# Two transformer blocks in one kernel: where the steps that make the modulation vectors are issued

## The chip, the core and the metric

The kernel runs on one core of a Trainium2 chip. The metric is device time in microseconds (us). Three runs of the kernel before took 2303.86, 2305.15 and 2305.77 us, so its median is 2305.15 us.

## The reference, cut to what matters

Two transformer blocks of two layers each run one after the other on 512 latent tokens of 1024 features (the first block also on 256 context tokens). Every layer begins with a norm whose result is scaled and shifted by *modulation vectors*, and ends with a gate that is one too. All modulation vectors come from one small vector `c` (in the first block also `c_ctx`) and large matrices, and depend on nothing else:

```python
for l in range(DEPTH):                    # first block
    mod_l = (silu(c) @ ada_w[l] + ada_b[l])           # [6 * 1024]
    mod_c = (silu(c_ctx) @ ada_w[l] + ada_b[l])
    sh1, sc1, g1, sh2, sc2, g2 = split(mod_l, 6)
    xl = xl + g1 * mixer(rms_norm(xl, norm_mix_w[l]) * (1 + sc1) + sh1)
    xl = xl + g2 * conv_ffn(rms_norm(xl, norm_ffn_w[l]) * (1 + sc2) + sh2)
for l in range(DEPTH):                    # second block
    sh, sc, g = split(silu(c) @ ada_w_2[l] + ada_b_2[l], 3)
    x = x + g * attention(rms_norm(x, norm_g_2[l]) * (1 + sc) + sh)
```

That makes 18 vectors of 1024 numbers: `(0, ...)` and `(1, ...)` with six names each for the first block's layers, `(2, ...)` and `(3, ...)` with sc, sh and g for the second block's. Those of layer 0, and (1, sc1) and (1, sh1), have two columns (`c` and `c_ctx`), the others one.

## The kernel before, in words

Tokens lie along the free dimension and features along the 128 partitions, in 8 chunks. All products are float32 made of two parts: a weight block and an activation are each split into a high part (wH, hH) and a low part (wL, hL), and TensorE adds up three products of them (L333).

**Weights.** They lie in DRAM in the order of their use, in blocks of 512 KB. `Stream.load` (L67 to L73) brings a block into one of 5 buffers of the tag `raw`; `Stream.prep` splits it, wH by ScalarE (L85) and wL by VectorE (L86), into one of 4 pairs. A block is split one block ahead of its use, and each split is followed by a further load. All loads are issued by SP, in one order.

**The stages, in order.** `mixer0`; `ffn(0)` on 768 tokens (feed-forward layer 0); `mixer1`; `ffn(1)` on 512 tokens (layer 1); `even2`, the first attention of the second block; `odd2`, the second. A feed-forward layer goes through the 2816 hidden features in three groups (8, 7, 7 blocks of 128): the up-projection `lin("up...")`, then the down-projection `lin("dn...")`. The last down-projection works by parts of the tokens, and as each part is done, the next layer's norm of that part follows (`norm`, `after`, L461 to L463: n_t and hL on VectorE, hH on ScalarE). The first two blocks of a layer's first product also go by parts. The attentions are 8 units each; `overlap` (L1065) emits unit i and, behind it in priority, the products that unit i + 1 needs. The softmax of a unit goes from TensorE (scores) to VectorE (L1139), ScalarE (L1140), VectorE (P, L1248 or L1287), TensorE (transposes, L1130) and both (ptH, ptL), then to TensorE again.

**The modulation vectors.** They are made in 144 steps. A step loads a tile of 512 KB of a matrix (`ada_load`, L242) into one of the same 5 `raw` buffers. The first 40 steps are done by TensorE in `mixer0` (`ada_pe`). The other 104 are those of the generator `ada` (L290): 13 vectors of 8 steps, with 4 steps for each half of a vector. A step holds two chunks of the matrix's rows. For each chunk ScalarE multiplies the tile by the chunk's scalars (L308, and L304 for a half's first chunk), and GpSimd adds it to an accumulator `gacc` (L309); where a vector has two columns, VectorE does the first column's part (L306). After the fourth step four small products for each column by TensorE sum over the partitions (L316), and VectorE turns the result (L318) and adds the bias (L257, L264).

**When a step is issued.** `mm` counts in `self.pe` TensorE's time as columns / 2400 us. `run` emits the work; behind each chunk of a product it asks whether `pe` has reached `ada_next`, and if so it emits a step and sets `ada_next = pe + every`. `ada_pace(9.2)` is set at a feed-forward layer's start (L699) and `ada_pace(inf)` at its end (L713), `ada_pace(11.0)` in `even2` (L1324), where it stays. `ada_until(keys)` emits at once the steps that are still missing for the vectors named: in `ffn` ahead of each down-projection (L706), in `even2` (L1326) and `odd2` (L1427) ahead of the last unit, there for (2, g), (3, sc), (3, sh) and for (3, g).

The order in which it is emitted is a priority: a scheduler orders every engine's instructions by it, as far as what each needs is there by its estimate. So a step's load or products can run well before the product behind which they were emitted. On the chip each engine then works in that fixed order.

```python
    def run(self, *gens):                              # L388
        for g in gens:
            for _ in g:
                while self.pe >= self.ada_next:
                    next(self.ada_gen, None)
                    self.ada_next = self.pe + self.ada_every
```

Of the kernel before, what the change touches and what calls it, by code (L numbers as in the profile page):

```python
# [21 lines left out]
KD = 8  # L22
# [4 lines left out]
NF = DFF // 128  # L27
# [20 lines left out]
class Stream:  # L48
    """Weight blocks in the order of their use, loaded ahead and split into two float32r parts."""
# [47 lines left out]
    def take(self, tag, ahead=None):  # L97
        """The next block's parts; the blocks behind it are made ready first."""
        i = self.used
        assert self.blocks[i][0] == tag, (tag, self.blocks[i])  # L100
        self.ahead(1)
        self.used += 1
        self.ahead(self.kk.AHEAD if ahead is None else ahead)
        return self.ready.pop(i)


class Banks:
    """A product's token runs, each in a bank of PSUM that is taken when it is first named."""
# [14 lines left out]
class Kern:  # L123
# [42 lines left out]
    def psum(self, parts, **banks):  # L166
        """Who takes which of the banks, in turn, from here on; parts: who, by part of the tokens."""
        self.banks, self.turn = {**self.BANKS, **banks}, dict.fromkeys(self.BANKS, 0)
        self.parts = parts
# [64 lines left out]
    def ada_load(self, pool=None, bufs=0):  # L234
        """Step (m, b, n, k, d): of vector m the blocks of 128 columns b .. b + n, of its matrix the rows k .. k + d."""
# [16 lines left out]
    def ada_put(self, m, b, n, value, nv):  # L252
        """The modulation vector's blocks b .. b + n have their product: value."""
# [15 lines left out]
    def ada_pe(self, n):  # L269
        """The next n steps of modulation vectors, by TensorE."""  # L270
# [19 lines left out]
    def ada(self):  # L290
        """The modulation vectors: sums over the chunks of the rows by GpSimd, over the partitions by TensorE."""
# [30 lines left out]
    def ada_pace(self, every):  # L322
        self.ada_every, self.ada_next = every, self.pe + every
# [12 lines left out]
    def lin(self, tag, nb, hH, hL, segs, evac, first=None, last=None, after=None):  # L336
        """Feature-major blocks: psum[m, t] = sum_k W[k, m] h[k, t]; the first or last two by parts of the tokens,
        after(part) when the last two have had one."""
# [27 lines left out]
    def lin_tm(self, tag, pairs, hH, hL, nt, evac):  # L366
        """Token-major blocks of 256 columns: psum[t, m] = sum_k h[k, t] W[k, m]."""
# [15 lines left out]
    def split(self, src, h, l):  # L383
        """h + l = src, each a float32r."""
# [3 lines left out]
    def run(self, *gens):  # L388
        """Emits the gens; among them, as TensorE's time passes, the modulation vectors' steps."""
        for g in gens:  # L390
            for _ in g:
                while self.pe >= self.ada_next:
# [4 lines left out]
    def merge(main, fill, per):  # L397
        """Runs main; behind each of its steps, fill's for about that much time on TensorE."""
# [10 lines left out]
    def pipeline(steps):  # L409
        """Steps of (elementwise, TensorE, what reads PSUM): each stage one step behind the one before."""  # L410
# [12 lines left out]

    def rsqrt(self, pool, r, x, n, scratch=None):
        """r = (x / n + eps) ** -0.5 =: v ** -0.5, by a step of Newton's: y (3 - 4 v y y), y about v ** -0.5 / 2."""
# [10 lines left out]
    def rstd_from(self, pool, rstd, sq, segs, n):  # L436
        """rstd[p, t] = (sum_p sq[p, t] / n + eps) ** -0.5 on all partitions."""
# [5 lines left out]
    def norm(self, name, side, T, x, A, B):  # L443
        """A modulated norm of x(j, s, e), by parts of the tokens: add() takes a chunk whose values are there, after()
        makes the part's H + L once all its chunks are."""
# [21 lines left out]
    def sumsq(self, pool, T, x):  # L467
        """add(j, s, e): takes chunk j's squares; rstd(part): the tokens' 1 / rms, on all partitions."""
# [174 lines left out]

    def ffn(self, l, T, segs, parts, n, x, nxt, side):
        """Adds to the chunks x(j, s, e); n: their norm; nxt opens the next layer's."""
# [53 lines left out]
        self.ada_pace(9.2)  # L699
# [19 lines left out]

    def mixer1(self, n):  # L720
# [19 lines left out]
        def raw_evac(raw, acc):  # L740
            """Copies block b to raw[b] and adds its squares to acc."""
# [63 lines left out]
    def out_proj(self, tag, y, gate, side, done, nxt):  # L805
        """x += gate * (y @ w); done: the pools to close when y has been split; nxt opens the next norm."""
# [21 lines left out]
    def rotate(self, pool, x, rope):  # L828
        """x: 64-feature heads [128, 512]; each pair of 16-feature runs turned by its angles."""
# [37 lines left out]
    def mla_in(self, tmp, keep, scratch, qlH, qlL, kvH, kvL, qp, rope):  # L867
        """The heads' queries, keys and values by token, the first two normalised but for their weights; qp[h]:
        the turned part of the queries, by feature, [high; low] or [low; high]."""
# [6 lines left out]
        def unit(*parts):  # L876
            """Each (x, nt, n): the heads of n features of nt tiles of tokens, over their rms."""
# [68 lines left out]
    def mla(self, raw, y, qpe, kpH, kpL, first):  # L946
# [8 lines left out]
        def weighted(h, x, nt, w, tag):  # L955
            """[tokens, 128] tiles -> w times their features by token, as a float32r pair: steps."""
# [107 lines left out]
    def overlap(self, n, produce, attend, first=(), last=None):  # L1064
        """Attends to unit i, behind it in priority what produces unit i + 1; last() before the last unit."""  # L1065
# [951 lines left out]
```

## Time and profile before

| | |
|---|---|
| median of three runs | 2305.15 us (2303.86 to 2305.77) |
| the profiled execution: span from first to last instruction | 2305.6 us |
| TensorE busy | 2199.9 us, 95% of the span |
| VectorE busy | 1542.2 us, 67% |
| ScalarE busy | 1118.7 us, 49% |
| GpSimd busy | 407.4 us, 18% |
| mean granted clock of TensorE | 0.985 |
| bytes read from HBM | 222.46 MB, 97 GB/s over the span |

What lies around the span is not shown apart: the span is within the three runs' times, 0.45 us above their median. A granted clock of 1.00 is 2.4 GHz, of 0.50 is 1.2 GHz. "PE" is TensorE's matmul, "PEld" its weight load, DVE is VectorE, ACT is ScalarE, POOL is GpSimd, SP issues the loads. A busy TensorE is not one at its peak: matmuls are pipelined, and their ends are modelled.

### The profile page before, as it was taken

The page shows a single profiled execution, that of the slowest core. Times are in us where ns is not written, and L with a number is a line of the kernel's source. Part 1 is how long each engine was busy: PE and PEld are TensorE (multiplying, and loading weights), DVE is VectorE, ACT ScalarE, POOL GpSimd, SP SyncE. Part 2 cuts the span into 40 slices and gives each one's busy share as a digit, 9 for nine tenths or more (in the row PEclk, how much of TensorE's full clock was granted, in tenths as well). Part 3 has the DMA queues.
Part 4 walks back from the last instruction along what each step waited for, and adds up shares of the span by engine and source line. Part 5 has one row for each costly group of instructions (what it writes and reads, how often), then busy time and mean ns, then how long its engine had stood idle before and what let it go on. Part 6 is the DMA issues. An engine that isn't in the chain of part 4 may idle for free.

```text
span 2305.6 us, 34273 instructions
## 1 busy us (share of the span) xinstructions
PE 2199.9 (95%) x13243; PEld 1880.2 (82%) x13243; DVE 1542.2 (67%) x2938; ACT 1118.7 (49%) x2124; POOL 407.4 (18%) x389
## 2 busy tenths in 40 slices
PE   6899899989999999999999999999999989989997
PEld 4788798788888888888889878878788877778886
DVE  5867775486545544547798675454567867968996
ACT  5444443254423423334577454343446756746773
POOL 0323321012122221221000013222211122101110
PEclk9999999999999999999999999999999999989999
DMA  9111111713333334331220134445434232213111
GB/s 322 65 47 32 33 56 38 283 56 125 106 117 110 113 107 128 105 115 59 76 92 1 46 119 138 145 131 155 137 108 137 80 95 92 73 56 95 56 46 37
DMA packets 86708, 226.78 MB, mean 98 GB/s; under 512 B 7184, under 2 KB 15376, under 8 KB 86544
## 3 DMA queue, kind: packets, MB, share of 16 engines
q1 hardware_dynamic: 86544, 224.58, 30.6%
q8 instruction: 104, 1.70, 0.3%
q14 instruction: 60, 0.49, 0.1%
HBM read 222.46 MB, written 2.10 MB: 97 GB/s over the span
## 4 chain that ended last, share of the span: by engine, by line
PE 75%; DVE 15%; ACT 5%; issue 2%; DMA 2%; POOL 1%; SPq 0%; DVEq 0%; ACTq 0%; POOLq 0%
PE b L333 72%; DVE wL L86 2%; DMA raw<-in_ada_w_dram 2%; DVE hL L463 1%; DVE n_t L461 1%; PE b L1130 1%; ACT wH L85 1%; PE b L280 1%; DVE s L1139 1%; DVE ptL L386 1%; PE b L1018 1%; DVE ksL L1092 1%; DVE n_acc L478 0%; PE b L316 0%; ACT ptH L385 0%
## 5 line engine op out<-in xcount | busy, mean ns | idle before, releaser
L333 PE MATMUL b<-hH,wH 128*128 128x256 f32 (+1 forms) x1880 | 597.6, 359 | 15.3 <-ACT hH L462 8.0
L333 PE MATMUL b<-hH,wL 128*128 128x256 f32 (+1 forms) x1880 | 593.5, 357 | 3.6 <-DVE wL L86 3.6
L333 PE MATMUL b<-hL,wH 128*128 128x256 f32 (+1 forms) x1880 | 588.9, 356 | 2.9 <-DVE hL L463 2.8
L309 POOL TENSOR_TENSOR gacc<-gacc,raw 128x512 f32<-128x512 f32 x182 | 261.5, 1437 | 1002.6 <-ACT raw L308 971.5
L333 PEld LDWEIGHTS b<-hH,wH 128*128 128x128 f32 x1880 | 356.0, 191 | 70.6 <-ACT hH L462 9.6
L333 PEld LDWEIGHTS b<-hH,wL 128*128 128x128 f32 x1880 | 357.6, 191 | 52.8 <-DVE wL L86 4.2
L333 PEld LDWEIGHTS b<-hL,wH 128*128 128x128 f32 x1880 | 355.5, 191 | 53.7 <-DVE hL L463 3.9
L86 DVE TENSOR_TENSOR wL<-raw,wH 128x1024 fp32r<-128x1024 f32 (+2 forms) x270 | 341.9, 1268 | 73.9 <-ACT wH L85 73.2
L85 ACT ACTIVATE wH<-raw 128x1024 fp32r<-128x1024 f32 (+2 forms) x270 | 278.1, 1031 | 176.0 <-PE b L333 173.4
L308 ACT ACTIVATE raw<-raw,csil 128x512 f32<-128x512 f32 x182 | 125.6, 717 | 202.4 <-DMA raw<-in_ada_w_dram 134.1
L333 PE MATMUL b<-hidH,wH 128*128 128x512 f32 (+1 forms) x563 | 167.8, 345 | 0.0
L333 PE MATMUL b<-hidH,wL 128*128 128x512 f32 (+1 forms) x563 | 167.4, 344 | 0.0
L333 PE MATMUL b<-hidL,wH 128*128 128x512 f32 (+1 forms) x563 | 167.2, 344 | 0.0
L333 PE MATMUL b<-yH,wH 128*128 128x256 f32 (+1 forms) x408 | 129.5, 334 | 5.1 <-ACT yH L385 4.9
L333 PE MATMUL b<-yH,wL 128*128 128x256 f32 (+1 forms) x408 | 129.5, 333 | 1.5 <-DVE wL L86 1.5
L333 PE MATMUL b<-yL,wH 128*128 128x256 f32 (+1 forms) x408 | 129.5, 334 | 0.0
L668 DVE TENSOR_SCALAR a<-gp,vecs 128x769 f32<-128x769 f32 (+1 forms) x44 | 39.1, 888 | 123.9 <-ACT gp L664 123.9
L333 PEld LDWEIGHTS b<-hidH,wH 128*128 128x128 f32 x563 | 105.5, 188 | 14.5 <-issue 1.2
L333 PEld LDWEIGHTS b<-hidH,wL 128*128 128x128 f32 x563 | 105.8, 188 | 13.6
L333 PEld LDWEIGHTS b<-hidL,wH 128*128 128x128 f32 x563 | 105.8, 188 | 13.1
L385 ACT ACTIVATE ptH<-b 128x384 fp32r<-128x384 f32 (+2 forms) x160 | 77.7, 500 | 64.7 <-PE b L1130 49.0
L333 PE MATMUL b<-wH,hH 128*128 128x256 f32 x352 | 100.9, 288 | 2.7 <-ACT z L519 1.5
(366 smaller groups left out, 3938.9 us busy)
## 6 DMA issues: line engine op xcount, KB each, us to landing
raw<-in_weights_dram SPq DMA_DIRECT2D x231, 512.0 KB, 3.5
raw<-in_ada_w_dram SPq DMA_DIRECT2D x144, 512.0 KB, 3.9
raw<-in_weights_dram SPq DMA_DIRECT2D x32, 448.0 KB, 3.3
x0t<-in_xT_dram SPq DMA_DIRECT2D x4, 768.0 KB, 7.0
xlat<-in_xT_dram SPq DMA_DIRECT2D x2, 1024.0 KB, 10.2
out_dram<-fo SPq DMA_DIRECT2D x8, 256.0 KB, 2.3
raw<-in_weights_dram SPq DMA_DIRECT2D x3, 384.0 KB, 3.0
xctx<-in_xT_dram SPq DMA_DIRECT2D x2, 512.0 KB, 7.0
```

What stands on the lines that cost most here:

```text
L85: nc.scalar.activation(h[:, :n], src, AF.Copy)
L86: nc.vector.tensor_tensor(l[:, :n], src, h[:, :n].bitcast(F32), op=ALU.subtract)
L280: nc.tensor.matmul(acc[32 * q:32 * q + 32, :], self.csil[:, k + a, :], raw[:, a, :, q, :], start=k + a == 0, stop=k + a == KD - 1)
L308: nc.scalar.activation(raw[:, a], raw[:, a], AF.Copy, scale=c)
L309: nc.gpsimd.tensor_tensor(acc[v], acc[v], raw[:, a], op=ALU.add)
L333: self.nc.tensor.matmul(ps, lhsT, rhs, start=start, stop=stop, **kw)
L385: self.nc.scalar.activation(h, src, AF.Copy)
L386: self.nc.vector.tensor_tensor(l, src, h.bitcast(F32), op=ALU.subtract)
L461: nc.vector.scalar_tensor_tensor(t, x(j, s, e), A[:, j, v:v + 1], r, op0=ALU.mult, op1=ALU.mult)
L463: nc.vector.scalar_tensor_tensor(hL[j][:, s:e], t, b, h.bitcast(F32), op0=ALU.add, op1=ALU.subtract)
L668: nc.vector.tensor_scalar(a, gp[:, 1:1 + L], cw(1, i), cb(i), op0=ALU.mult, op1=ALU.add)
L1018: nc.tensor.transpose(ps[:, c], P[:, a, c], self.ident)
```

## The change

In a feed-forward layer the pace is 7.2 in place of 9.2. The first step may come 8 us later than it could before, and none comes in the layer's last 16 us (by `self.pe`, and `total` is the layer's count). `even2` sets no pace any more, so that after layer 1 it stays at infinity, and only the demands of `ada_until` emit steps. Docstrings and comments also go, which changes no instruction.

```diff
-    def ada_pace(self, every):
-        self.ada_every, self.ada_next = every, self.pe + every
+    def ada_pace(self, every, start=0.0, end=math.inf):
+
+        self.ada_every, self.ada_next, self.ada_end = every, self.pe + start + every, self.pe + end
...
     def run(self, *gens):
...
         for g in gens:
             for _ in g:
-                while self.pe >= self.ada_next:
+                while self.ada_next <= self.pe < self.ada_end:
                     next(self.ada_gen, None)
                     self.ada_next = self.pe + self.ada_every
...
     def ffn(self, l, T, segs, parts, n, x, nxt, side):
...
-        self.ada_pace(9.2)
+        total = 3 * NF * KD * 3 * T / 2400
+        self.ada_pace(7.2, 8.0, total - 16.0)
         i0 = 0
...
     def even2(self, n):
...
-        self.ada_pace(11.0)
         def last():
             self.ada_until((2, "g"), (3, "sc"), (3, "sh"))
             self.close("h_b0")
```

## Rows read from the trace of the kernel before

**Rows 1.** Four stages: stretch, us, busy PE PEld DVE ACT POOL, granted clock, DMA share, GB/s
```profile
700.00:900.00 200.00, 200.00 (x1192) 174.47 (x1191) 94.36 (x106) 67.23 (x95) 47.99 (x33) 1.00 0.36 113
1500.00:1650.00 150.00, 150.00 (x665) 119.40 (x665) 79.80 (x90) 60.82 (x85) 35.37 (x24) 1.00 0.47 142
1760.00:2000.00 240.00, 228.20 (x1135) 180.56 (x1134) 191.91 (x405) 166.30 (x317) 45.89 (x30) 0.99 0.30 92
2060.00:2250.00 190.00, 188.51 (x1068) 157.72 (x1067) 173.38 (x509) 135.72 (x358) 25.97 (x48) 1.00 0.20 63
```

**Rows 2.** The additions of L309 alone in even2: stretch, us, POOL busy, clock, DMA
```profile
1745.00:2000.00 255.00, 39.09 (x28) 0.99 0.30 94
```

**Rows 3.** The chain of waits: a group of small products in layer 1
```profile
1374.72 0.36 PE b L316 x8
```

**Rows 4.** Who made TensorE wait from 1760 to 2010: us in total, times, longest
```profile
PE b L333 <- DVE sm L1139: 4.1, 2, 3.2
PE b L1130 <- DVE P L1287: 2.5, 4, 0.9
PE b L333 <- DVE vb L386: 1.7, 1, 1.7
PE b L1130 <- DVE sm L1281: 1.1, 1, 1.1
```

**Rows 5.** ScalarE's timeline in even2: start, us, operation [idle before <-releaser]
```profile
1891.56 0.72 ACT L308 ACTIVATE raw<-raw,csil 128x512 f32<-128x512 f32 x1 [2.19 <-DMA raw<-in_ada_w_dram]
```

**Rows 6.** Short stretches after TensorE's waits, columns as in rows 1
```profile
1344.00:1348.00 4.00, 1.88 (x8) 1.79 (x9) 3.93 (x11) 1.31 (x3) 0.00 (x0) 0.50 0.74 248
...
1722.00:1726.00 4.00, 4.00 (x20) 3.92 (x21) 4.00 (x12) 1.92 (x5) 0.00 (x0) 0.58 0.12 46
1865.00:1870.00 5.00, 4.09 (x16) 3.67 (x17) 4.43 (x15) 3.17 (x7) 0.81 (x1) 0.66 0.17 68
1890.00:1895.00 5.00, 3.27 (x9) 2.05 (x8) 1.61 (x4) 2.70 (x7) 1.26 (x1) 0.67 0.49 154
```

**Rows 7.** VectorE's timeline at five places, alone and beside GpSimd's additions
```profile
507.68 1.66 DVE L463 SCALAR_TENSOR_TENSOR hL<-n_t,mods,hH 128x256 fp32r<-128x256 f32 x4
...
1336.95 3.52 DVE L463 SCALAR_TENSOR_TENSOR hL<-n_t,mods,hH 128x256 fp32r<-128x256 f32 x4
...
1710.99 1.32 DVE L478 TENSOR_TENSOR n_acc<-n_acc,n_sq 128x256 f32<-128x256 f32 x1 [0.54 <-ACT n_sq L477]
...
1718.45 1.38 DVE L433 TENSOR_TENSOR rsz<-rsz,rsm 128x256 f32<-128x256 f32 x1
...
1729.31 0.41 DVE L432 TENSOR_TENSOR rsz<-n_r 128x256 f32<-128x256 f32 x1
...
1837.43 1.48 DVE L1287 SCALAR_TENSOR_TENSOR P<-P,sm 128x512 f32<-128x512 f32 x1
...
1928.13 0.74 DVE L1287 SCALAR_TENSOR_TENSOR P<-P,sm 128x512 f32<-128x512 f32 x1
```

**Rows 8.** TensorE's timeline: the first products after four waits
```profile
518.71 0.58 PE L333 MATMUL b<-hH,wL 128*128 128x256 f32 x1 [3.28 <-DVE wL L86]
...
1346.12 0.58 PE L333 MATMUL b<-hH,wH 128*128 128x256 f32 x1 [2.83 <-ACT hH L462]
...
1719.61 0.43 PE L316 MATMUL b<-gacc,ones 128*32 128x128 f32 x8 [0.66 <-POOL gacc L309]
1721.89 0.38 PE L333 MATMUL b<-hH,wH 128*128 128x256 f32 x1 [1.85 <-ACT hH L462]
```

**Rows 9.** SP's timeline: loads of modulation matrices at the layers' starts
```profile
471.93 0.38 SPq L242 DMA_DIRECT2D raw<-in_ada_w_dram  x1
...
1330.67 0.38 SPq L242 DMA_DIRECT2D raw<-in_ada_w_dram  x1
...
1344.23 0.38 SPq L242 DMA_DIRECT2D raw<-in_ada_w_dram  x1
```

**Rows 10.** DMA issues: operation xcount, KB each, median us from issue to landing
```profile
raw<-in_ada_w_dram SPq DMA_DIRECT2D x144, 512.0 KB, 3.9
```

## The prediction

> **What bounds the kernel now.** The table by stage comes first. From 700 to 900 us (feed-forward layer 0) and from 1500 to 1650 us (layer 1) TensorE has not one idle microsecond, though the modulation steps run there: no other engine is near its limit, and only what stops TensorE or lowers its clock costs time. From 1760 to 2000 us (the first attention of the second block, "even2") it idles 240 - 228.2 = 11.8 us, and steps run there too; in the second attention ("odd2", 2060 to 2250), built alike and without steps, 1.5 us in 190 [rows 1]. After that I read who makes TensorE wait [rows 4], what the queues of ScalarE and VectorE do just before those waits [rows 5, 7], and the same at layer 1's two ends, where a norm ties TensorE to VectorE: there it idles again, and the granted clock falls to 0.5, the 1.2 GHz level [rows 6, 8].
>
> A step is a 512 KB load by SP, two products on ScalarE, two additions on GpSimd; every fourth adds a group of small products on TensorE.
>
> **How many steps go where.** The emitter counts TensorE's time in chunks, of 0.96 us in layer 0 and 0.64 in layer 1, so a pace of 9.2 becomes 9.6 in both (10 and 15 chunks), and 7.2 becomes 7.68 (8 and 12). Of 144 steps, 40 are done ahead of layer 0. Before: 53 in layer 0 (52 by the pace, one by the demand ahead of the last down-projection), 35 in layer 1, 16 in even2. The trace agrees: 28 additions from 1745 to 2000 us [rows 2], and four half vectors have 7 each. After: layer 0 counts 506.88 us; its first step comes at 15.36 (8.0 + 7.2, up to the next chunk) and the last before 490.88, which makes 62. Layer 1 counts 337.92 us, from 15.36 to 321.92: 40. That is 102 of 104. The last two, of the vector (3, g), are left to the demand ahead of odd2's last unit. So +9, +5, -16, and +2 in odd2, which had none: the change does not quite do what its name says.
>
> **even2.** Three things go with its 16 steps. (1) ScalarE's queue is in order: before 1891.56 a step's product had made it wait 2.19 us for its landing, the copies of vb stood behind it [rows 5], and TensorE waited 1.7 us for vb [rows 4]. (2) GpSimd's additions stretch VectorE: a 512-column update of P takes 0.74 us alone and 1.48 beside an addition, 0.74 more [rows 7]. (3) Four groups of products, 0.36 us each on the chain [rows 3], 1.4 in all. The waits that I tie to steps, since an addition or a landing stands beside the last links before them, are those for sm of L1139, P, vb and sm of L1281: 4.1 + 2.5 + 1.7 + 1.1 = 9.4 us [rows 4], 80% of the 11.8. The two longest lower the clock: 0.66 and 0.67 in two stretches of 5 us, 3.3 us lost, of which some 0.9 falls on idle already counted: 2.4 [rows 6]. I take 9.4 and 80% of the 2.4, less 0.5, since odd2 has some idle too: 10.8, with the groups **-12.2**. Bounds: all of it, -11.8 - 2.4 - 1.4 = -15.6, and +1 (the same idle for other reasons, in a new order of instructions).
>
> **End of layer 1.** Two steps run while the last down-projection turns into the next norm. Beside their additions three short operations of VectorE take about 1.35 us each (first and third shown: 1.32, 1.38), where 0.41 is usual: 2.8 us on the chain that TensorE waits for [rows 7]. It idles 0.66 us for an addition itself and 1.85 for the norm [rows 8], then runs at clock 0.58 for 4 us, 1.7 us lost [rows 6]. Now the last step comes 24 us of TensorE time before the layer's end, not 3. What is late next is the norm's second half, VectorE's work in one piece; so I gain what VectorE gains, 2.8, and some of the clock: **-3.5**. Bounds: 0, and -(0.66 + 1.85 + 1.7 + 0.36) = -4.6.
>
> **Start of layer 1.** The first step's load is issued at 1330.67 [rows 9]; its additions stretch four hL from 1.66 to 3.52 us [rows 7], and TensorE then waits 2.83 us [rows 8] and falls to clock 0.50 [rows 6]. In the new order this step stands behind one more weight block: the first two end at 10.24 us, the third at 15.36. SP takes the steps' and the weights' loads in one order, so the load goes about where the second step's went, 1344.23 [rows 9]. VectorE gains 1.9 us and ScalarE a little: **-2.2**. Bounds: 0, and the wait with half of the 1.88 us that ran at half clock, -2.83 - 0.9 = -3.8.
>
> **Start of layer 0.** Here the 8 us buy nothing. Steps 1 to 4 stood at 9.6, 19.2, 28.8 and 38.4 us, within blocks 0-1, 2, 3 and 4; now they stand at 15.36, 23.04, 30.72 and 38.4, the ends of the same blocks. Each load follows the same weight load as before, and the first goes out at 471.93, ahead of the layer [rows 9]. So the additions stay where they are, and so does the wait of 3.28 us for a weight's low part [rows 8]: **0**. Bounds: -5 (this wait, and a clock loss like the 1.7) and +1.9 (one more pair of additions, as at layer 1's start). At layer 0's end the norm has no addition beside it: 0.
>
> **Inside the layers.** 14 more steps are 3.5 groups of 0.36 us [rows 3]: **+1.3**, since TensorE is full. The loads, products and additions I cost at nothing: in 200 us of layer 0 VectorE is busy 94.4, ScalarE 67.2, GpSimd 48.0 [rows 1]. In layer 0's up-projections a step now falls on every block's end; one in four or five did before, without a wait. If that cover is gone, see the first rival.
>
> **odd2.** Two steps, where VectorE is busy 173.4 of 190 us [rows 1]. Their loads wait in SP's order behind the output projection's first blocks, and put its last ones off; those are needed last. Price of a step in even2: (11.8 + 2.4) / 16 = 0.9; two of them and a group, 1.8 + 0.4: **+2.2**. Bounds: 0.4, and both landings exposed at 3.9 us each with the group, 8.2 [rows 10].
> The Trainium skill (SBUF — State Buffer, section "Who interferes with whom") holds that only the port pair which VectorE and GpSimd share causes contention, and that it is an exclusive lock. By that rule an addition can hold VectorE for its whole 1.3 us or so, not 0.74 as the row has it; four of them would make the odd2 term up to 5.2 + 0.4, and the sum 2294.
>
> **The sum.** -12.2 - 3.5 - 2.2 + 0 + 1.3 + 2.2 = -14.4. The profiled execution's span is 2305.6 us, 0.45 above the median of the runs (2305.15): 2305.6 - 14.4 - 0.45 is 2290.75, say **2291**.
>
> **Rivals.**
> *The layers can't hide it (slower).* Steps and weights share five load buffers and SP's one order, so a step that is late delays weights. If a block's low part then comes late in layer 0, TensorE waits as it does at 518.71, 3.28 us [rows 8]. This outweighs the gain from (14.4 + 1.3) / 102 = 0.15 us a step; at 0.3, one such wait in eleven steps, it adds 31: 2322. Against it: no idle at all in the 200 us of layer 0 or the 150 us of layer 1 [rows 1]. 8%.
> *even2's idle is not the steps'.* VectorE and ScalarE hand each softmax to and fro, and one wait would come for another. Then 1.4 of the 12.2 is won: 2291 + 10.8 = 2302. For it: each of these waits names VectorE's own softmax work, not a step [rows 4]. Against it: odd2 idles little. 18%.
> *odd2 pays in full.* Both landings fall on the last unit: 8.2 in place of 2.2, 2297. For it: VectorE has little slack there; against: the output projection's blocks are there to fill TensorE. 12%.
>
> **How the numbers follow.** The forecast keeps 62%. A measurement of this kernel tells some 0.2%, 4.6 us; the second rival, 3 us under the median, lies within that, with half its chance on either side. Faster: 0.62 x 0.98 + 0.18 x 0.5 + 0.12 x 0.85 = 0.80; same: 0.01 + 0.08 + 0.02 = 0.11; slower: the first rival and a little, 0.09. Range: even2, layer 1's ends and layer 0's start at the better bounds give -3.4 - 1.1 - 1.6 - 5; not all come together, and 10 of these 11 make 2281. The high end takes in the other two cases: 2302.
>
> **What would show it.** Right: short VectorE operations at layer 1's end and no addition there; no step in even2, idle there under 4 us and no half clock; a first wait in layer 1 under 1 us; layer 0's start as it is; two steps in odd2 before its last unit. Wrong: waits for wL or for evacuations inside the layers, or idle of 8 us and more in even2 without steps.

## The result, and the profile after

The changed kernel takes 2337.89 us (median of 4 runs, 2332.78 to 2339.23) against 2305.46 for the kernel before on the same chip: 1.3% slower, ratio 1.0132 with a 95% interval of 1.0117 to 1.0146. The forecast was 2291, 0.6% faster. The profiled execution took 2339.23 us, its span is 2337.5 us.

To see where the time went I cut both spans at five marks on GpSimd, which stand at the same places of the work: the clearing of layer 0's buffers (gp), the first sum of squares of mixer 1 (kvr), the clearing of layer 1's buffers, the first bias made from dist (even2) and the first from band (odd2).

| stage | before, us | after, us | difference | predicted |
|---|---|---|---|---|
| layer 0, to mixer 1's first sum | 592.8 | 627.4 | **+34.6** | +0.8 |
| mixer 1 | 252.6 | 252.7 | +0.1 | 0 |
| layer 1, to even2's bias | 408.5 | 413.3 | **+4.8** | -5.2 |
| even2, to odd2's bias | 344.8 | 333.1 | -11.7 | -12.2 |
| odd2, to the end | 218.3 | 221.8 | +3.5 | +2.2 |

(0.8 and -5.2 divide the +1.3 inside the layers by steps, 9 to 5.) What was to be gained in even2 was gained. All of the loss, and more, lies in layer 0, which I had costed at next to nothing.

The table by stage of the changed kernel, with the four stretches of [rows 1] moved to where the same work now stands (columns as there: stretch, us, busy PE PEld DVE ACT POOL, granted clock, DMA share, GB/s):

```profile
700.00:900.00 200.00, 190.54 (x1106) 162.89 (x1105) 82.24 (x90) 65.47 (x94) 54.90 (x37) 0.99 0.34 114
1536.00:1686.00 150.00, 146.30 (x641) 115.54 (x640) 79.72 (x93) 62.96 (x88) 39.75 (x29) 0.98 0.48 151
1800.00:2040.00 240.00, 234.95 (x1165) 189.08 (x1165) 194.31 (x415) 152.75 (x297) 7.87 (x3) 1.00 0.19 62
2095.00:2285.00 190.00, 185.82 (x1039) 154.04 (x1039) 174.63 (x509) 136.87 (x361) 31.10 (x52) 1.00 0.21 68
```

Read it against [rows 1]. In layer 0 TensorE now idles 9.5 of 200 us, though VectorE and ScalarE are *less* busy than before (82.2 against 94.4 us, 65.5 against 67.2). No engine is near its limit; the work has become slower as a whole. So the next view is the chain of waits (the work that ended last, followed back from link to link); its summary on the page, the shares of the span by line:

```profile
PE b L334 51%; DMA raw<-in_ada_w_dram 12%; DVE wL L86 4%; ACT raw L308 2%; ACT wH L85 2%; POOL gacc L309 2%; PE b L1132 1%; DVE n_t L462 1%; DVE hL L464 1%; DVE a L669 1%; PE b L280 1%; ACT gp L665 1%; PE b L1020 1%; DVE ksL L1094 1%; DVE n_acc L479 0%
```

The steps' loads hold 12% of the chain that sets the end, and from 700 to 900 us the shares are these, first of the kernel before, then of the changed one:

```profile
by line: PE b L333 98.9%; PE b L316 1.1%
```

```profile
by line: DMA raw<-in_ada_w_dram 47.5%; issue 11.5%; DVE wL L86 8.7%; ACT raw L308 8.6%; ACT wH L85 6.5%; POOL gacc L309 5.9%; ACT gp L665 2.3%; DVE a L669 2.2%; DVE a L670 1.9%; ACT gacc L304 1.1%; ACT a L672 0.8%; DVE hidL L387 0.8%; DVE h
```

TensorE's own work, all of the chain before, is off it in this stretch. The chain itself, piece by piece (start, us, what), shows what runs there instead:

```profile
828.11 4.06 DMA raw<-in_ada_w_dram
...
832.91 0.71 ACT raw L308
833.62 0.85 ACT wH L85
834.47 0.02 issue
834.49 1.09 DVE wL L86
835.59 1.59 DVE hidL L387
837.17 4.86 DMA raw<-in_ada_w_dram
...
842.76 0.71 ACT raw L308
843.47 0.85 ACT wH L85
844.33 0.05 issue
844.37 2.23 POOL gacc L309
846.61 0.02 issue
846.62 0.33 SPq L71
...
847.04 4.87 DMA raw<-in_ada_w_dram
```

It is a closed loop. A step's load lands after 4 to 5 us; ScalarE makes the products; behind them in its queue stands a weight split; then either VectorE's split (wL) or GpSimd's addition (gacc) frees a load buffer; SP issues a weight load into it (L71 at 846.62, the instant the addition ends) and right behind that the next step's load (847.04). The next round begins only when this one is done. (In the first of the two rounds the chain passes through hidL, but there too the additions end at 836.72 us by GpSimd's timeline, and the weight load goes out at 836.75.) The loads of steps between 748.60 and 893.90 us are 9.69 us apart (15 rounds); before, from 743.13 to 895.82, they were 10.18 apart. Over the longer stretch from 754 to 1040 us it is 9.68 after and 10.78 before.

SP's own waits show the same from the other side (engine, line, what it waited for: us in total, times, longest us). From 560 to 1040 us before:

```profile
SPq L71 <- POOL gacc L309: 120.6, 34, 4.5
SPq L71 <- DMA raw<-in_ada_w_dram: 89.0, 25, 4.5
```

and from 560 to 1060 us after:

```profile
SPq L71 <- POOL gacc L309: 149.5, 41, 8.8
SPq L71 <- DMA raw<-in_ada_w_dram: 128.4, 33, 5.4
```

L71 loads *weights*. It waits for the landing and the additions of *steps*, since the buffer that it gets is one that a step has just had. That stood in the trace of before; it cost nothing there, as the next view shows. These are TensorE's waits from 560 to 1060 us after the change; before there was none from 560 to 1040:

```profile
PE b L334 <- ACT gp L665: 14.5, 8, 6.1
PE b L334 <- DVE xctx L694: 3.6, 2, 2.2
PE b L334 <- DVE hidL L387: 2.8, 2, 1.4
PE b L334 <- ACT hidH L386: 1.3, 1, 1.3
PE b L334 <- DVE xlat L694: 0.4, 2, 0.2
```

22.6 us, none of it for a weight's low part: weights come late to ScalarE and VectorE, the evacuations of PSUM stand behind them in both queues, and TensorE waits for the banks. The first of these waits is at 754 us, some 265 us after the layer's start. I take it that the loads' lead is used up until then; no view here shows that lead.

### The profile page after: what moved, and what is told of

Read it like the earlier page. It is cut to its first block, busy times and chain, and to the rows that moved or that the text cites. A ratio compares the mean times of both kernels' runs of the same rounds, so it can differ in the third digit from the quotient of the medians.

```text
span 2337.5 us, 34283 instructions
## 1 busy us (share of the span) xinstructions
PE 2209.2 (95%) x13243; PEld 1883.4 (81%) x13243; DVE 1556.8 (67%) x2938; ACT 1117.1 (48%) x2124; POOL 403.6 (17%) x389
## 4 chain that ended last, share of the span: by engine, by line
PE 55%; DVE 17%; DMA 12%; ACT 9%; issue 5%; POOL 2%; SPq 0%; ACTq 0%; DVEq 0%; POOLq 0%
PE b L334 51%; DMA raw<-in_ada_w_dram 12%; DVE wL L86 4%; ACT raw L308 2%; ACT wH L85 2%; POOL gacc L309 2%; PE b L1132 1%; DVE n_t L462 1%; DVE hL L464 1%; DVE a L669 1%; PE b L280 1%; ACT gp L665 1%; PE b L1020 1%; DVE ksL L1094 1%; DVE n_acc L479 0%
## 5 line engine op out<-in xcount | busy, mean ns | idle before, releaser
L334 PE MATMUL b<-hH,wH 128*128 128x256 f32 (+1 forms) x1880 | 603.2, 361 | 31.4 <-ACT gp L665 14.7
L334 PE MATMUL b<-hH,wL 128*128 128x256 f32 (+1 forms) x1880 | 594.7, 358 | 3.7 <-DVE wL L86 3.7
L334 PE MATMUL b<-hL,wH 128*128 128x256 f32 (+1 forms) x1880 | 591.3, 358 | 2.3 <-DVE hL L464 2.0
L86 DVE TENSOR_TENSOR wL<-raw,wH 128x1024 fp32r<-128x1024 f32 (+2 forms) x270 | 350.3, 1300 | 159.7 <-ACT wH L85 159.1
L334 PEld LDWEIGHTS b<-hH,wH 128*128 128x128 f32 x1880 | 357.1, 191 | 91.3 <-ACT gp L665 20.0
L334 PEld LDWEIGHTS b<-hH,wL 128*128 128x128 f32 x1880 | 358.2, 191 | 52.9 <-DVE wL L86 4.2
L334 PEld LDWEIGHTS b<-hL,wH 128*128 128x128 f32 x1880 | 355.8, 191 | 53.4 <-DVE hL L464 2.8
L309 POOL TENSOR_TENSOR gacc<-gacc,raw 128x512 f32<-128x512 f32 x182 | 258.2, 1419 | 793.4 <-ACT raw L308 772.9
L334 PE MATMUL b<-hidH,wH 128*128 128x512 f32 (+1 forms) x563 | 169.0, 346 | 4.9 <-ACT hidH L386 2.4
L334 PE MATMUL b<-hidL,wH 128*128 128x512 f32 (+1 forms) x563 | 167.5, 344 | 3.2 <-DVE hidL L387 3.2
L334 PE MATMUL b<-hidH,wL 128*128 128x512 f32 (+1 forms) x563 | 168.1, 345 | 0.0
L669 DVE TENSOR_SCALAR a<-gp,vecs 128x769 f32<-128x769 f32 (+1 forms) x44 | 44.1, 1001 | 151.9 <-ACT gp L665 151.9
L334 PE MATMUL b<-yH,wH 128*128 128x256 f32 (+1 forms) x408 | 130.1, 336 | 5.2 <-ACT yH L386 5.2
L334 PE MATMUL b<-yH,wL 128*128 128x256 f32 (+1 forms) x408 | 129.6, 333 | 1.5 <-DVE wL L86 1.5
L334 PE MATMUL b<-yL,wH 128*128 128x256 f32 (+1 forms) x408 | 130.3, 335 | 0.4 <-DVE yL L387 0.4
L334 PEld LDWEIGHTS b<-hidH,wH 128*128 128x128 f32 x563 | 105.6, 188 | 21.0 <-issue 3.9
L334 PEld LDWEIGHTS b<-hidL,wH 128*128 128x128 f32 x563 | 106.1, 189 | 17.4 <-DVE hidL L387 4.3
L334 PEld LDWEIGHTS b<-hidH,wL 128*128 128x128 f32 x563 | 106.2, 189 | 13.2
L334 PE MATMUL b<-wH,hH 128*128 128x256 f32 x352 | 100.4, 286 | 2.5 <-ACT z L520 1.5
```

The costliest lines, as they stand in the source:

```text
L86: nc.vector.tensor_tensor(l[:, :n], src, h[:, :n].bitcast(F32), op=ALU.subtract)
L309: nc.gpsimd.tensor_tensor(acc[v], acc[v], raw[:, a], op=ALU.add)
L334: self.nc.tensor.matmul(ps, lhsT, rhs, start=start, stop=stop, **kw)
L669: nc.vector.tensor_scalar(a, gp[:, 1:1 + L], cw(1, i), cb(i), op0=ALU.mult, op1=ALU.add)
```

## The experiments

Twelve kernels, all compared by the stages above ("the mark" is the first sum of squares of mixer 1); each ratio is to the kernel before in the same session, whose median was between 2305 and 2308 us. The stage times are each of one profiled execution, while whole runs of the kernel before spread from 2299.6 to 2311.4 us, so a difference of 2 or 3 us in a stage is not shown by itself. Every kernel was also ordered anew by the scheduler, so no run changes a buffer and leaves all else in its place. The theories: **L**, later **R**: the closed loop through the load buffers. **G**: GpSimd's additions harm by stretching VectorE's operations. **P** and **T**: steps are too dense, or stand at a bad place of the block, whatever the buffers.

| kernel | median us | ratio to before (95%) | layer 0 | layer 1 | even2 | odd2 |
|---|---|---|---|---|---|---|
| before | 2305.46 | | 592.8 | 408.5 | 344.8 | 218.3 |
| changed | 2337.89 | 1.0132 (1.0117-1.0146) | 627.4 | 413.3 | 333.1 | 221.8 |
| own2 | 2299.76 | 0.9972 (0.9962-0.9981) | 589.4 | 411.7 | 335.9 | 221.4 |
| ahead | 2342.39 | 1.0154 (1.0139-1.0169) | 626.6 | 413.2 | 333.4 | 221.7 |
| vec_add | 2292.18 | 0.9937 (0.9923-0.9952) | 591.0 | 404.1 | 332.6 | 222.0 |
| pace82 | 2312.41 | 1.0019 (1.0008-1.0030) | 598.0 | 406.4 | 339.6 | 229.4 |
| free | 2307.00 | 1.0004 (0.9993-1.0015) | 605.9 | 403.7 | 332.8 | 221.0 |
| slots4 | 2324.20 | 1.0081 (1.0057-1.0106) | 620.9 | 405.0 | 335.0 | 220.2 |
| before_vec | 2299.35 | 0.9972 (0.9962-0.9981) | 589.8 | 408.2 | 339.2 | 219.0 |
| vec_none_left | 2293.13 | 0.9946 (0.9932-0.9959) | 595.3 | 403.3 | 333.5 | 218.6 |
| phase | 2327.46 (one run) | | 626.8 | 405.0 | 333.6 | 221.7 |
| before_hold | 2403.07 (one run) | | 651.9 | 433.3 | 355.4 | 218.1 |
| vec_best | 2290.10 | 0.9920 (0.9906-0.9934) | 590.3 | 403.8 | 333.4 | 218.7 |
| vec_best_own | 2287.38 | 0.9911 (0.9897-0.9926) | 588.3 | 405.4 | 333.5 | 218.0 |

**own2: buffers of their own for the steps' loads**, in each layer up to its last down-projection.

```
-            t = (pool or self.ring).tile([128, 1024], F32, name="raw", tag="raw", bufs=bufs or self.SLOTS)
+            t = (pool or self.ada_own[0]).tile([128, 1024], F32, name="raw", tag="raw", bufs=bufs or self.ada_own[1])
...
-        i0 = 0
+        i0, self.ada_own = 0, (self.open("ax", "left" if side == "right" else "right"), 2)
...
```

> The steps' loads get two buffers of their own during each feed-forward layer (up to its last down-projection), the weights keep the five. Mark used: GpSimd's first norm-square addition of mixer 1 (1081.4 us before, 1116.6 after). Theory L (closed loop: a step's load waits for the weight split that frees a shared buffer, ScalarE's in-order queue waits for its landing, the next weight split stands behind it): the loop is opened, the mark comes back to 1081-1090, ScalarE's waits for landings in 560-1060 us fall from 185 to under 90 us, and the kernel is 25 to 40 us faster than the changed one (2298-2313 us). Theory P (a step on every block's end is too dense for the engines, whatever the buffers) and theory G (GpSimd's additions stretch VectorE): mark stays above 1105, time within 8 us of 2338.

The mark came back to 1078.5, 3 us earlier than in the kernel before (and 2.5 below the range expected), with the same 62 steps and every addition still on GpSimd. The table by stage, 600 to 900 us, of the changed kernel and then of own2:

```profile
600.00:900.00 300.00, 290.54 (x1717) 250.02 (x1716) 139.82 (x159) 102.23 (x143) 85.17 (x58) 0.99 0.35 116
```

```profile
600.00:900.00 300.00, 300.00 (x1800) 261.04 (x1799) 148.59 (x170) 117.14 (x162) 107.22 (x70) 1.00 0.42 132
```

GpSimd does *more* additions in this stretch (70 against 58), and TensorE does not idle at all; the chain of waits from 700 to 900 us is TensorE's own work again (98.9% L334, 1.2% L316). That is the end of G and P, as causes by themselves, for layer 0. SP's waits say what is gone; of own2, 560 to 1060 us:

```profile
SPq L71 <- POOL gacc L309: 15.4, 4, 4.5
SPq L71 <- DMA raw<-in_ada_w_dram: 15.0, 4, 4.3
```

15.4 and 15.0 us in place of 149.5 and 128.4. ScalarE's waits for landings fell from 140.4 + 44.4 to 78.4 + 7.7 us, as expected. Layer 1 stayed slow here, 411.7; that is another matter, below.

**ahead: each step's load issued one step earlier, in the shared buffers.**

```
             raw = self.ada_take()
+            if self.pe + self.ada_every + 1 < self.ada_end:
+                self.ada_load()
```

> The changed kernel, but each step's load is issued one step earlier, in the same ring of five buffers. Theory L, if the landing on ScalarE's queue is what closes the loop: landings are hidden, the mark (first norm-square addition of mixer 1) comes back under 1090 and the time to 2300-2313. Theory L, if the shared buffers close it: the extra load holds a fifth of the ring, the mark stays above 1105 or gets worse. Theory G: mark stays above 1105.

Mark 1116.9, as in the changed kernel, and ScalarE still waits 160.4 us for landings, in place of 184.8. Asking earlier does not help where the buffer comes from the round before.

**vec_add: the steps' additions on VectorE.**

```
-                        nc.gpsimd.tensor_tensor(acc[v], acc[v], raw[:, a], op=ALU.add)
+                        nc.vector.tensor_tensor(acc[v], acc[v], raw[:, a], op=ALU.add)
```

> The changed kernel with the steps' additions on VectorE in place of GpSimd; loads, products and buffers as they are. Theory G (the additions on GpSimd stretch VectorE's evacuations): the mark (first norm-square addition of mixer 1) comes back under 1095. Theory L: ScalarE's waits for landings stay over 150 us in 560-1060 us and the mark stays at 1105-1130.

By the expectation as written this was G's: the mark came back to 1079.9. I had not counted the addition as a link of the loop. It is one: the buffer is free only when it is done, and on VectorE it takes half the time. First the changed kernel, then vec_add (operation, count: ns min/median/max, first and last start, forms):

```profile
L309 POOL TENSOR_TENSOR gacc<-gacc,raw x96: 1263/1300/2229, 559.4 to 1054.2; 128x512 f32<-128x512 f32 x96
```

```profile
L309 DVE TENSOR_TENSOR gacc<-gacc,raw x94: 649/692/694, 577.3 to 1017.9; 128x512 f32<-128x512 f32 x94
```

Weight loads then wait for additions 39.4 us in 18 waits, not 149.5 in 41, and TensorE is full. But GpSimd's additions beside VectorE's work are gone too, so this run alone could not tell G from the loop; own2 and free, which keep them, do. I restated L as R, with the addition in the loop.

**pace82: 9 chunks between steps, not 8.**

```
-        self.ada_pace(7.2, 8.0, total - 16.0)
+        self.ada_pace(8.2, 8.0, total - 16.0)
```

> The changed kernel with a pace of 8.2 in place of 7.2, which the chunks make 8.64 of counted time in layer 0 (9 chunks) and 8.32 in layer 1 (13): 55 steps in layer 0, 37 in layer 1, 12 left for the demands of the second block. Theory L: the loop's round of 9 to 10 us is about the real 8.64 x 1.097 = 9.5 us, so layer 0 loses most of its waits: mark 1081-1095. Theory P by density alone: in proportion, 55 of the way from 53 to 62 steps, about +8 us: mark 1085-1095. Theory T (it is the step's phase on the block's end that hurts): with 9 chunks a step no longer falls on every block's end, mark 1081-1084. The steps left over come in one burst ahead of the second block's last units: even2 longer than in the changed kernel by 10 to 25 us.

Layer 0 took 598.0 us, 5.2 more than before: with 10, 9 and 8 chunks between steps the loss is 0, 5.2 and 34.6 (the profiled run of pace82 was the slowest of its seven, 2.8 us over their median, and TensorE's waits in it from 560 to 1060 us are 3.2 us). The mark, 1085.5, lies in the ranges of both L and P and so does not tell these two apart (2 of the 9 added steps would be 7.7 us by density); it is just outside T's. Even2 and odd2 took up the steps left over, 6.5 and 7.6 us more than in the changed kernel; for even2 I had written 10 to 25.

**free: the product goes into a tile of its own**, so that the load buffer is free before GpSimd adds.

```
-                        nc.scalar.activation(raw[:, a], raw[:, a], AF.Copy, scale=c)
-                        nc.gpsimd.tensor_tensor(acc[v], acc[v], raw[:, a], op=ALU.add)
+                        p = self.ada_prod.tile([128, 512], F32, name="prod", tag="prod", bufs=4) if self.ada_prod else raw[:, a]; nc.scalar.activation(p, raw[:, a], AF.Copy, scale=c)
+                        nc.gpsimd.tensor_tensor(acc[v], acc[v], p, op=ALU.add)
...
```

> The changed kernel with one thing else: during a feed-forward layer (up to its last down-projection) ScalarE writes a step's product into a tile of its own, not back into the load buffer, so that the buffer is free as soon as ScalarE has read it and not only after GpSimd's addition. GpSimd makes the additions as before. Theory R (GpSimd's slow addition is a link of the closed loop through the five shared load buffers): mark (first norm-square addition of mixer 1; 1081.4 before, 1116.6 after) at 1078-1090, weight loads wait for GpSimd's additions under 40 us in 560-1060 us in place of 149.5, total 2296-2312. Theory G (the additions harm by stretching VectorE's own operations): they stay where they are, so mark above 1105 and total above 2325.

Mark 1094.6: 22 of the 35 us are back, where G allowed none, with GpSimd's additions all in place. The rest stays, a miss against the 1090 that I had written. The chain in this kernel shows why (start, us, what): without GpSimd's link the loop still closes, through the weight split that stands behind the product.

```profile
828.48 3.78 DMA raw<-in_ada_w_dram
...
832.97 0.71 ACT prod L308
833.68 0.85 ACT wH L85
834.53 0.02 issue
834.56 1.10 DVE wL L86
835.66 0.02 issue
835.68 4.49 DMA raw<-in_ada_w_dram
```

Rounds are 8.83 us here from 742.73 to 892.89 us. In vec_add, where TensorE is full and so sets the time between steps, they are 8.46 from 748.96 to 892.74.

**slots4: four shared buffers in place of five.**

```
-    SLOTS = 5
+    SLOTS = 4
```

> The changed kernel with four shared load buffers in place of five. Theory R: a load then waits for a buffer used four loads ago and not five, the loop gets longer for each step: mark well above the changed kernel's 1116.6, 1135 or more, total over 2360. Theory G and theory P (density alone): buffers do not matter, mark 1112-1121.

R, as I had put it, missed: 1109.5, 7 us *earlier* than with five buffers, and also 2.5 below the range of G and P. One buffer fewer does not make the loop longer. SP's waits are nearly what they were (weight loads for additions, 153.5 us in 42 waits, with five 149.5 in 41). I read this so: a load is not given the buffer of five loads ago but one that the schedule has coming free then, and with steps and weights taking turns that is often the last step's.

**phase: the same steps in the middle of a block.**

```
-        self.ada_pace(7.2, 8.0, total - 16.0)
+        self.ada_pace(7.2, 12.0, total - 16.0)
```

> The changed kernel with a start of 12.0 in place of 8.0: as many steps in layer 0 (62) and the same pace, but each falls in the middle of a block and not on its end. Theory R: the round of load, product and additions is what it was, mark 1108-1125. Theory T (a step on every block's end collides with the block's evacuation): most comes back, mark under 1097.

Layer 0 took 626.8 us, in place of 627.4, and the mark is at 1114.0: T falls, in one run. What the whole gained, 10 us, lies in layer 1 and is taken up below.

**before_hold: the kernel before, with the buffers held longer.**

```
                         nc.gpsimd.tensor_tensor(acc[v], acc[v], raw[:, a], op=ALU.add)
+                        nc.gpsimd.tensor_tensor(raw[:, a], raw[:, a], raw[:, a], op=ALU.add)
```

> The kernel before, at its old pace, with a second GpSimd operation of 512 columns on a step's load buffer behind each addition (its value is not read), which holds the buffer some 1.3 us longer for each of a step's two halves. Mark: GpSimd's first norm-square addition of mixer 1, 1081.4 in the kernel before. Theory R (a weight load that takes the buffer of the step ahead of it waits for its landing, product and additions, and the next step's load stands behind it): the round of 9.0 to 9.9 us grows to about 12, more than the 10.5 us between steps at the old pace, so the old pace loses too: mark at 1091 or later, TensorE waits inside layer 0 (560-1040 us) where there were none. If the hold does not matter: mark within 3 us of 1081.4, no waits there. (Even2 gets longer in either case; it is not read.)

The other way round it works too: the mark is at 1141.7, 60 us later, at the old pace, in one run. The loads of steps are 11.92 us apart from 742.66 to 897.59 (10.18 before), TensorE waits inside layer 0 (for gp alone 22.6 us from 560 to 1060; the kernel before has no wait from 560 to 1040), and SP's largest wait from 560 to 1060 us is

```profile
SPq L71 <- POOL raw L310: 183.3, 31, 8.3
```

This run does not hold the buffer alone: it also puts twice as much of GpSimd's work beside VectorE's, which G would charge for as well.

**before_vec: the kernel before with additions on VectorE.** (The diff is that of vec_add.)

> The kernel before with the steps' additions on VectorE, pace and places as they were. It splits the prediction's even2 term: if its idle is GpSimd's additions stretching VectorE (term 2 of even2), even2 (dist bias to band bias, 344.8 us before) falls by 4 to 8 us; if it is the landings in ScalarE's queue (term 1) or the groups, by under 3. Theory R: layer 0 and layer 1 unchanged within 2 us, since the loop has slack at this pace; total 2297-2306.

Even2 fell by 5.6 us, about half of what the change gains there, though VectorE now makes the additions itself; the other half I put down to the rest of the step. TensorE's waits for sm and P (1757 to 2007 us) fall to 1.7 us, those for ptL rise to 3.6. The run also gives the load buffers back earlier, and does not tell this from what the additions do to VectorE. Layer 0 gained 3.0, a little more than the 2 that I had allowed.

**vec_none_left, vec_best, vec_best_own: the change with the loop open.** All have additions on VectorE and make all 104 steps in the layers, 64 in layer 0 and 40 in layer 1; the first has no start in layer 0, the second keeps it, the third has own2's buffers too.

```
-        self.ada_pace(7.2, 8.0, total - 16.0)
+        self.ada_pace(7.2, *((0.0, total - 8.0) if l == 0 else (8.0, total - 16.0)))    # vec_none_left
+        self.ada_pace(7.2, 8.0, total - (7.0 if l == 0 else 16.0))                      # vec_best, vec_best_own
```

> The changed kernel with additions on VectorE and, in layer 0, no start and an end of 8 us, so that layer 0 makes 64 steps, layer 1 40, and none is left for the second block. Theory R: mark 1079-1083 in spite of two more steps, since the loop is open; odd2 (band bias to end, 222.0 in the run with additions on VectorE) shorter by 3.0-3.7, since its two steps are gone; total 2286-2291. Rival: odd2's 3.5 us are not the steps' but the order's: odd2 stays at 221-222, total 2291-2294.

> As the run with additions on VectorE and none left, but with the start of 8 us kept in layer 0 and an end of 7 us there: again 64 steps in layer 0, 40 in layer 1, none after. It tells whether the start of 8 us in layer 0 bought something (I had put it at 0): if so, mark 1079.5-1081.5, as with 62 steps (1079.9), and total 2288-2291; if the start buys nothing and the two further steps cost the 3.5 us, mark 1083-1084.5 and total 2291-2294, as without the start.

> As the run before this one, and the steps' loads have two buffers of their own in each feed-forward layer. Theory R: no weight load waits for a step's buffer, and layer 0 gains what own buffers gained with GpSimd's additions (-3.4 in place of -1.8 with VectorE's): mark 1077.5-1081; layer 1 (memset to dist bias) 403-405.5; total 2285-2291. If the schedule's bunching of loads does harm in layer 1 as in the run with own buffers (411.7): total 2292-2299.

The first came out at 2293.13, above its range (its mark, 1083.4, too), the other two within theirs, but for the last one's mark, 1075.2, which is earlier than its range. Odd2 fell from 222.0 to 218.6 us without its two steps. Layer 0 lost 4.3 without the start of 8 us and got 5.0 back with it, at the same 64 steps (3.0 by the medians). Own buffers make layer 0 2.0 shorter and layer 1 1.6 longer, which is within what single executions differ by. The last kernel is the fastest, 2287.38 us, 0.9% under the kernel before, and faster than the changed one by 50 us.

## Why the prediction was wrong

**The step that failed** is "inside the layers": "The loads, products and additions I cost at nothing: in 200 us of layer 0 VectorE is busy 94.4, ScalarE 67.2, GpSimd 48.0." [Rows 1] are true, and they answer another question. They say that the engines have time; what limited layer 0 was not an engine's time but the length of one round through SP, a landing, ScalarE's queue, an addition and a buffer, in which each waits for the last. No busy share shows such a round. The forecast had +0.8 us for layer 0, and it was +34.6; own2, free and vec_add, which open the round at three places, give back 38.0, 21.5 and 36.4 us of layer 0.

The size is consistent with such a round, but the rows do not derive it. The changed kernel's rounds take 9.69 us where vec_add, with TensorE full, asks for a step every 8.46: 1.23 us too long, and 29.5 of them from 754 to 1040 us make 36 us, against +34.6 measured. But a step is emitted every 8 chunks of TensorE's own work, so whatever holds TensorE stretches this distance by as much, and the agreement says nothing of the cause. It also hangs on the stretch: from 754 to 1040 us the steps' loads are 10.78 us apart before, 9.68 after and 8.73 in vec_add. By these the old pace had 1.1 us of slack a round, which the waits of SP before (120.6 + 89.0 us) could fill without cost, and the new pace asked for 2.05 less. Nine chunks, at 9.7 to 9.8 us, should then have cost next to nothing, and pace82 was 5.2 us longer. Nor has the round one fixed length: from 562 to 749 us the changed kernel's loads are 8.48 us apart, and TensorE does not wait. Why the loop binds only from there on stays open.

In TensorE's own time, the stage has 23.2 us more idle (8.8 before, 32.0 after) and 11.4 us more busy time. The trace has as many of its products in both (3409 of L333 before, 3408 of L334 after), so none are missing: they took longer. Some 4 us of that at most is a lower granted clock (0.91, 0.88 and 0.95 in the 20 us from 760, 900 and 920); the rest is not placed.

**The rival named it.** "Steps and weights share five load buffers and SP's one order, so a step that is late delays weights": that is the mechanism, at 8%. Two things in it were off. TensorE does not wait for a block's low part but for evacuations, which stand behind the late splits. And its price, 2322, came from 0.3 us a step, taken from one wait in eleven steps, where layer 0 lost 34.6 us in 62 steps, 0.56 a step. What I held against it, no idle at all in the layers, is what a loop with slack looks like from TensorE. The view that speaks was SP's waits, which I had not asked for inside the layers: with 25 of the weight loads behind a landing of a step and 34 behind an addition, it was in the trace of before.

**Even2: right in the main, with some luck.** -11.7 for -12.2. It idles 5.1 of 240 us (under 4 was forecast), its granted clock is 1.00, and the waits for sm and P of [rows 4] have gone from 7.7 to 0.9 us. But the 1.7 us for vb, which I had tied to a landing in ScalarE's queue, stand there without any step (TensorE's timeline after):

```profile
1927.34 0.50 PE L334 MATMUL b<-hH,wH 128*128 128x512 f32 x1 [1.73 <-DVE vb L387]
```

So part (1) of even2 was read wrongly: of the 9.4 us tied to steps these 1.7 were not theirs. The idle of the 240 us fell by 6.7 us where 8.9 was forecast; what made up for the rest is not worked out. before_vec puts 5.6 us on the additions being GpSimd's, as [rows 7] showed in small.

**Odd2: right in kind, a third too small.** +3.5 for +2.2; 3.4 by the run without those steps, where the additions were VectorE's. The Trainium skill (SBUF — State Buffer, section "Who interferes with whom"), by which I had worked out up to 5.6 here from an exclusive lock, gave an upper figure, and 3.5 lies under it. This does not speak against the lock, and the trace agrees with it operation by operation. In layer 0 after the change, GpSimd's timeline and then VectorE's (start, us, operation):

```profile
764.30 2.66 POOL L309 TENSOR_TENSOR gacc<-gacc,raw 128x512 f32<-128x512 f32 x2 [6.48 <-ACT raw L308]
```

```profile
765.77 2.28 DVE L86 TENSOR_TENSOR wL<-raw,wH 128x1024 fp32r<-128x1024 f32 x1 [3.99 <-ACT wH L85]
```

The split starts while the second addition runs and ends 1.09 us after that has ended, at 766.96; in vec_add, without GpSimd's additions, no split takes more than 1.23 us. I read the 1.48 us of [rows 7] in the same way, as a wait for what is left of an addition and not as a slower speed: the addition beside that update of P ends at 1838.37, the update at 1838.91. It goes the other way too: the pair of additions from 833.13 takes 3.59 us, with a split of 1.09 us from 834.49 in between. Such waits are part of a round, and part of what vec_add takes out of it.

**Start of layer 1: right in size, but the sign named for it did not come.** A first wait under 1 us was to show it. The first block's last wait ends 10.15 us after the clearing of the buffers in place of 12.11, so 2.0 for 2.2, but not by the wait's going: TensorE now waits 3.79 us in one piece, where before it waited five times and 2.83 us at the longest [rows 8]. VectorE's timeline just before (start, us, operation):

```profile
1374.38 0.41 DVE L430 TENSOR_SCALAR rsm<-b 128x256 f32<-128x256 f32 x1
1374.71 2.34 DVE L86 TENSOR_TENSOR wL<-raw,wH 128x1024 fp32r<-128x1024 f32 x2
1376.98 0.41 DVE L433 TENSOR_TENSOR rsz<-n_r 128x256 f32<-128x256 f32 x1
```

```profile
1379.42 0.58 PE L334 MATMUL b<-hH,wH 128*128 128x256 f32 x1 [3.79 <-ACT hH L463]
```

Two weight splits stand in the middle of the norm's short operations. They stood there before, too (1341.13 and 1342.99, 1.21 us each); what has gone is the stretched hL ahead of them, the 1.9 us of the forecast, so I read the wait as theirs and not the additions'.

**End of layer 1: wrong.** -3.5 was forecast. The additions are gone, and VectorE's short operations take 0.42 us as foreseen, not the 1.4 of [rows 7]; but three weight splits of 1.23 us now stand between them, where before there was one (1715.13):

```profile
1756.76 1.23 DVE L86 TENSOR_TENSOR wL<-raw,wH 128x1024 fp32r<-128x1024 f32 x1 [0.61 <-ACT wH L85]
1757.90 0.42 DVE L479 TENSOR_TENSOR n_acc<-n_acc,n_sq 128x256 f32<-128x256 f32 x1
...
1759.24 1.23 DVE L86 TENSOR_TENSOR wL<-raw,wH 128x1024 fp32r<-128x1024 f32 x1 [0.18 <-ACT wH L85]
...
1761.70 1.23 DVE L86 TENSOR_TENSOR wL<-raw,wH 128x1024 fp32r<-128x1024 f32 x1 [0.18 <-ACT wH L85]
1762.85 0.42 DVE L479 TENSOR_TENSOR n_acc<-n_acc,n_sq 128x256 f32<-128x256 f32 x1
```

TensorE waits 2.74 us for the last n_acc. From the layer's last evacuation (1719.76 before, 1760.72 after) to even2's first key stack (1738.9, 1779.3) it takes 19.1 and 18.6 us: 0.5 won. Two further splits, 2.5 us, have taken most of the 2.8 us that the additions gave back. I asked what the additions stretch and not what would be next in VectorE's queue. That the splits hold the norm up is read from the queue's order; no run moved them. (By the forecast's own count the last step comes 23.0 us before the layer's end and before the change 1.9, not 24 and 3.)

**Inside layer 1.** Where phase, free and vec_add take 403.7 to 405.0 us, the changed kernel takes 413.3 and own2 411.7. The loop does not decide here: phase has the changed kernel's buffers and pace and is fast, own2 has buffers apart and is slow. Of TensorE's 4.7 us of waits inside the layer 3.1 are for a group of small products that stands in its queue ahead of the last addition, the longest this:

```profile
1541.64 0.42 PE L316 MATMUL b<-gacc,ones 128*32 128x128 f32 x8 [2.18 <-POOL gacc L309]
```

In the 20 us around it, and in the 20 from 1600, the granted clock is 0.91, 3.6 us together. In own2 one group of these products waits 4.7 us, by the profile for VectorE's hf (L681). In phase and vec_add TensorE has no wait from 1400 to 1700 us. Where the schedule puts these groups differs between kernels with the same pace, so this loss is not the pace's alone; what decides it was not tried.

**Start of layer 0.** As forecast, the change left it as it was: TensorE is busy 113.5 of the 120 us from 440 to 560 after, 113.4 before. But "here the 8 us buy nothing" is wrong where the loop is open: vec_best gets 5.0 us from them (3.0 by the medians).

**Counts.** All as forecast: 62 steps, 40, none, and two in odd2, at 2237.3 us and behind.

## What to carry to other kernels

Before a pace is raised, look for a loop, not only for busy engines: follow one item from its issue through its landing, each in-order queue and the buffer that it gives back to the next issue, add up the round, and compare it with the pace. A loop with slack costs nothing and looks like free engines; once the pace asks for less than a round takes, the engine that was full is held to the round. The waits of the queue that issues loads show it, even in a kernel where the bounding engine never idles; and loads of two kinds that share buffers and a queue wait for the slower kind's whole life, which two buffers of their own, or a faster last reader, undo.

## What was not expected of the hardware

One fewer load buffer was no slower but 14 us faster (slots4, two runs), some 6 us of it in layer 0 and 8 in layer 1. And in the same place, beside VectorE's work, a GpSimd addition of 512 columns took from 1263 to 2229 ns, median 1300, where VectorE's took 649 to 694: moved to the engine that is the busier of the two, the additions made TensorE wait nowhere inside either layer (560 to 1060 and 1400 to 1700 us).
